# First loads in a fixed order, a mask on GpSimd, a gate factor in output rows, w_out in freed buffers, and the memory stage later

## Chip, cores and metric

One core of a Trainium2 chip runs the kernel. The metric is the device time of one execution in microseconds (us). TensorE is called PE here, VectorE DVE, ScalarE ACT, GpSimd POOL and SyncE SP; all DMAs of this kernel are issued by SP.

## What is computed

One layer of a decoder trunk for 2048 prompt tokens and 64 sample tokens of width 1024. In short:

```
z = rmsnorm(x) @ w_in          # columns: a_x | a_o | a_i, a_f | b_u | b_g
u = b_u * sigmoid(b_g)         # head group B: conv of width 31, layernorm, silu
ha = sigmoid(a_o) * headnorm(mlstm(conv4(a_x), a_i, a_f), a_hnorm)   # head group A
x = x + concat(ha, cb) @ w_out
mk, mv = rmsnorm(mem) @ x_wk, rmsnorm(mem) @ x_wv                    # 256 memory tokens
x = x + cross_attention(rmsnorm(x), mk, mv) @ x_wo
x = rmsnorm(x + convffn(rmsnorm(x)))
```

The mLSTM works in chunks of 128 tokens. Inside a chunk it needs, for each of 4 heads, a 128x128 matrix of decays: the exponential of a per-row term plus a per-column term, and zero above the diagonal. The output gate's sigmoid is computed as (tanh(x/2) + 1) / 2.

## The kernel before, in words

Every float32 product is three float32r matmuls (`mm3`, L153): each operand is split into a high part, an ACT cast or scaled copy, and a low part, a subtraction (`split`, L295). With a gain the low part is a scalar_tensor_tensor on DVE (L301); without one it is a subtraction on the engine that the caller names, DVE or POOL (L298).

**First pass** (loop at L588): 8 blocks of 256 tokens. `input_part` (L548) loads the rows, normalises and transposes them into the block's `h` (tiles `ha` and `hb` in turn) and stores `h` to DRAM. `gates_part` (L380) makes the gate columns, `gates_tm_part` (L393) turns them. `glu_part` (L406) makes b_u and b_g with the weights `wgt` and `wbv` (8 pieces of 256 KB each, `load_in` at L324, through 6 raw buffers) and stores `u`. In it ACT halves b_u into `hu` (L423), and DVE multiplies by tanh + 1 (L424). The tiles `tg`, `gT` and `ot` share one ring of two buffers, tag "tg" (L390, L418, L432); `ot` is stored to DRAM from its buffer (L435). `late_part` (L584, L366) loads and splits weights of the second pass in between. The tile `hb` lies where the raw buffers of the first loads lay (L578, L579). The first loads that the pass does not need at once are the small vectors (L563 to L570), the q, k, v maps (L453), and, in `first_loads` (L337), the gate columns and the conv states, which are transposed and stored again (`us`, L359).

**Second pass** (loop at L1273): `rest_part` (L1188) reads `h` back and makes a_x and the output gate (`wa`, `wo_` in pools wp2, wp2b); the gate tile `tg` gets (tanh + 1) times half the head-norm gain on DVE (L1222) and goes to DRAM; `head_out` (L728) multiplies it in. `pre_part` (L1246) calls `decay` (L761): 4 scalar_tensor_tensor on DVE per chunk add the per-row term and take the minimum with a mask tile `cap` (L764), then one ACT exponential of 128x512 (L768). `recur` (L781) is the chain from chunk to chunk. `conv_block` (L663) is the width-31 conv: ACT products, POOL additions (`cside`, L646), DVE scalar_tensor_tensor (`psG`, L648). `head_tail` uses DVE, ACT and POOL.

**The end of the second pass.** After the last `rest_part` (ch == 7, L1278) the pool wa2 closes. `memory_kv` (L984), the stage that makes mk and mv, then runs step by step inside the last chunks (`fold` in `steps`, L1265), and w_out is loaded in 16 pieces through 2 raw buffers into pools opened there (L1156 to L1161, L1282, L1302). `out_part` (L1173) is the product with w_out for 128 tokens, 17 in all: 14 in the loops at L1296 and L1308, then the sample tokens and two more (L1313, L1579, L1587) beside the **fold** of the attention weights (`fold_values` L1127, `fold_keys` L1073). Attention and the feed-forward follow.

The order on each engine and on the DMA queue is set at build time by the Tile framework, which takes instructions by program order and by a simulated timeline. `high_priority` (L560) puts a block first.

Of the kernel before, what the change touches and what calls it, by code (L numbers as in the profile page):

```python
# [33 lines left out]
FOLD_STEPS = 1, 1, 2  # L34
# [7 lines left out]
WO_FIRST = 4  # L42
# [54 lines left out]
def trunk_kernel(ctx: ExitStack, tc: tile.TileContext, i: dict, o: list):  # L97
# [231 lines left out]
    for j in range(2):  # L329
        SY.dma_start(b8[:, j, :4], i["a_bi"][0].partition_broadcast(P))  # L330
        SY.dma_start(b8[:, j, 4:], i["a_bf"][0].partition_broadcast(P))
# [74 lines left out]
    def glu_part(ch, xts, h, n):  # L406
        if ch == 0:
            pgs = [mmps() for _ in range(H)]
            for k in range(KT):
                for c in range(H):  # L410
                    gemm_k(pgs[c], wgt, c * P, h, n, k)
        for c in range(H):
            if ch == 0:
                pg = pgs[c]
            else:
                pg = mmps()
                gemm_fm(pg, wgt, c * P, h, n)
# [34 lines left out]
    for j, key in enumerate(("a_wq", "a_wk", "a_wv")):  # L452
        SY.dma_start(wqkv[:, j], i[key][0].rearrange("h d e -> d h e"))  # L453
# [94 lines left out]
    def input_part(ch):  # L548
        xts = xts0 if ch == 0 else load_x(lambda t: xp[t * P:(t + 1) * P, :], xs, ch)
# [5 lines left out]
        n = CH + (S if ch == 0 else 0)  # L555
        for z in range(2):
            SY.dma_start(h_d[ch][:, :, z], f(h[:, z, :, :n]))
        return ch, xts, h, n
# [3 lines left out]
    wgt = load_in(1032 + DA, W_FIRST)  # L562
# [25 lines left out]
    for ch in range(NCH):  # L588
        cur_ = cur
        gates_part(*cur)  # L590
        if ch:
            glu_part(*cur)
            gates_tm_part(*cur)
        if ch + 1 < NCH:
            cur = input_part(ch + 1)
        if ch == 0:
            glu_part(*cur_)
            gates_tm_part(*cur_)
# [92 lines left out]
    h2p = wa2.enter_context(tc.tile_pool(name="h2", bufs=H2_BUFS, side="right", reuse_waits="tile"))  # L691
    ut2 = wa2.enter_context(tc.tile_pool(name="ut2", bufs=2, side="right", reuse_waits="tile"))
# [9 lines left out]

    cap = const01(m1, [P, P], "cap", 0.0, [([[1, P]], -1, 0, GE, NEG)])
# [24 lines left out]
    def head_out(nd, nt, to_src, cat, pool):  # L728
# [5 lines left out]
        tt(to, to, pt[:, :H * nt].rearrange("p (h t) -> p h t", h=H), ALU.mult)  # L734
# [26 lines left out]
    def decay(dm, k, q, pm, a, nt, capt, qi=None):  # L761

        for hh in range(H):
            stt(dm[:nt, hh, :nt], pm[:nt, hh * nt:(hh + 1) * nt], a[:, hh:hh + 1], capt, ALU.add, ALU.min)  # L764
# [3 lines left out]
        act(dm[:nt, :, :nt], dm[:nt, :, :nt], AF.Exp)  # L768
# [26 lines left out]
    def sample_mlstm():  # L795
# [4 lines left out]
        with tc.tile_pool(name="smp", bufs=1, reuse_waits="tile") as smp:  # L800
# [3 lines left out]
            cap_s = const01(smp, [S, NB, NS], "cap_s", 0.0, [(*x, NEG) for x in samb])  # L804
# [351 lines left out]
    def out_pool(name, k0, k1):  # L1156
        return wos.enter_context(tc.tile_pool(name=name, bufs=2 * (k1 - k0), side="right", reuse_waits="tile"))

    def load_out(wpo, k0, k1):
        return [load_w(wpo, i["w_out"][0][k * P:(k + 1) * P, :], eng=G, raws=(wpo0, 2))  # L1160
                for k in range(k0, k1)]  # L1161
# [22 lines left out]
    fold = memory_kv()  # L1184
# [3 lines left out]
    def rest_part(ch):  # L1188
# [29 lines left out]
        for c in range(H):  # L1218
# [3 lines left out]
            ts(tg[:, :n], tg[:, :n], 1.0, ALU.add, hnh[:, c:c + 1], ALU.mult)  # L1222
# [23 lines left out]
    def pre_part(ch, j):  # L1246
# [7 lines left out]
        decay(dm, k[:, :, c], q[:, :, c], mrs[ch][:, j], av[:, t], P, cap, qi)  # L1254
# [17 lines left out]
    outs = list(range(NT - 2))  # L1272
    for ch in range(NCH + 2):  # L1273
# [4 lines left out]
        if ch == NCH - 1:  # L1278
            wa2.close()
            wpo0 = out_pool("wpo0", 0, WO_FIRST)  # L1280
            next(fold)
            wout = load_out(wpo0, 0, WO_FIRST)  # L1282
        for j in range(2):
# [12 lines left out]
            if ch == NCH + 1:  # L1296
                for _ in range(2):
                    out_part(outs.pop(0))
        if ch == NCH:
            for _ in fold:  # L1300
                pass
            wout += load_out(out_pool("wpo1", WO_FIRST, KT), WO_FIRST, KT)  # L1302
            ctp = wos.enter_context(tc.tile_pool(name="ctp", bufs=CT_BUFS, side="right", reuse_waits="tile"))
# [4 lines left out]
    while outs:  # L1308
        out_part(outs.pop(0))
        steps(0)  # L1310
    for _ in side:
        pass
    ahead = [out_load(t) for t in (NT, NT - 2)]  # L1313
    out_part(NT, ahead[0])
# [262 lines left out]
    pps = banks("A", "A", "G", "D", "E")  # L1577
    with tc.tile_pool(name="fv", bufs=1, reuse_waits="tile") as fv:
        out_part(NT - 2, ahead[1])  # L1579
# [7 lines left out]
        out_part(NT - 1)  # L1587
        for j, _ in enumerate(fold):
            if j == ROWS_AT:
                next(keys)  # L1590
    next(keys)
    wos.close()
    wfs = ExitStack()
# [326 lines left out]
```

## Time and profile before

| | |
|---|---|
| median of 3 runs | 3009.47 us (3009.05 to 3010.59) |
| profiled execution, its own time | 3008.2 us |
| its span, first to last instruction | 3006.2 us |
| mean granted TensorE clock | 0.968 |
| PE busy | 2815.6 us (94%) |
| DVE busy | 2179.5 us (72%) |
| ACT busy | 1536.3 us (51%) |
| POOL busy | 1115.3 us (37%) |

Times are counted from the span's start. A row of the windows view gives, for a stretch, the time each engine was busy in it (with the number of instructions), the TensorE clock granted (1.00 is full speed), the mean busy share of the 16 DMA engines and what they moved. "PE x <- ACT y" means that PE stood idle before an instruction that writes x until ACT had made y.

### The profile page before, as it was taken

Reading aid. Unit: us, or ns where it says so; the run is one execution under the profiler, and the core shown is the slowest. Engines: PE = TensorE matmul, PEld = TensorE weight load, DVE = VectorE, ACT = ScalarE, POOL = GpSimd, SP = SyncE. Lnnn points to the kernel's source line nnn. Section 1 sums busy time; section 2 is a strip of 40 time slices with the busy share of each in tenths; the row PEclk is TensorE's granted clock in tenths of the full one; section 3 lists DMA queues with packets and bytes.
Section 4 is the critical chain, followed back from the end, with each engine's and each line's share of the span. In section 5 each row is a group of like instructions: output and inputs, shape, how many; then the busy total and the mean of one; then the engine's idle time right before and its main releaser. Section 6 shows DMA issues by size and latency. Waiting matters only on the chain.

```text
span 3006.2 us, 49437 instructions
## 1 busy us (share of the span) xinstructions
PE 2815.6 (94%) x17924; PEld 2483.7 (83%) x17924; DVE 2179.5 (72%) x4022; ACT 1536.3 (51%) x3115; POOL 1115.3 (37%) x1299
## 2 busy tenths in 40 slices
PE   5798989989999889899989999999999999999998
PEld 4687889987787778766678898899989999899987
DVE  3478899986212688844498889877797777877776
ACT  3467657777201565522364445655466545544443
POOL 2338745444310352533352323433253322522222
PEclk8898999999899999999989999999999999999999
DMA  7343333345644622556864454655465544644442
GB/s 194 104 150 114 126 114 118 110 127 189 204 156 150 226 73 95 200 178 224 275 213 155 155 173 152 219 163 161 137 225 163 160 151 148 190 135 127 129 122 75
DMA packets 336940, 471.81 MB, mean 157 GB/s; under 512 B 33421, under 2 KB 238707, under 8 KB 336688
## 3 DMA queue, kind: packets, MB, share of 16 engines
q1 hardware_dynamic: 336696, 468.66, 48.8%
q8 instruction: 141, 2.31, 0.3%
q14 instruction: 103, 0.84, 0.1%
HBM read 361.68 MB, written 107.26 MB: 156 GB/s over the span
## 4 chain that ended last, share of the span: by engine, by line
PE 70%; DVE 14%; DMA 8%; issue 3%; ACT 2%; POOL 2%; SPq 1%; DVEq 0%; POOLq 0%; ACTq 0%
PE psA L151 20%; PE psD L151 15%; PE psF L151 14%; PE psE L151 9%; PE psG L151 9%; DVE psG L125 3%; DMA raw<-in_f_wup 2%; DVE wt L128 2%; DMA raw<-in_w_in 1%; PE psB L148 1%; PE psC L148 1%; DMA h<-h 1%; DVE acc L125 1%; DVE raw L128 1%; DVE dm L125 1%
## 5 line engine op out<-in xcount | busy, mean ns | idle before, releaser
L297 ACT CAST wt<-raw 128x512 fp32r<-128x512 f32 x888 | 539.1, 620 | 545.2 <-PE psA L151 149.7
L128 DVE TENSOR_TENSOR wt<-raw,wt 128x512 fp32r<-128x512 f32 x662 | 511.9, 790 | 107.8 <-ACT wt L297 103.4
L128 POOL TENSOR_TENSOR wt<-raw,wt 128x512 fp32r<-128x512 f32 x226 | 319.9, 1420 | 718.7 <-ACT wt L297 603.8
L151 PE MATMUL psA<-R,wt 128*128 128x256 f32 (+1 forms) x2448 | 335.1, 287 | 2.9 <-DVE R L125 1.6
L151 PEld LDWEIGHTS psA<-R,wt 128*128 128x128 f32 x2448 | 315.2, 191 | 6.1 <-DVE R L125 1.8
L128 POOL TENSOR_TENSOR cside<-cside,cprod 128x512 f32<-128x512 f32 (+2 forms) x248 | 251.5, 1015 | 137.5 <-ACT cprod L120 94.4
L125 DVE SCALAR_TENSOR_TENSOR psG<-ue,vc,psG 128x512 f32<-128x512 f32 (+2 forms) x448 | 256.9, 573 | 13.3 <-ACT psG L120 5.6
L151 PE MATMUL psA<-wt,ht 128*128 128x512 f32 (+1 forms) x768 | 192.1, 396 | 0.0
L151 PE MATMUL psD<-R,wt 128*128 128x256 f32 (+1 forms) x1248 | 178.3, 288 | 11.6 <-DVE R L128 4.2
L151 PE MATMUL psF<-R,wt 128*128 128x256 f32 (+1 forms) x1248 | 177.8, 287 | 2.5 <-DVE R L125 1.7
L151 PE MATMUL psE<-R,wt 128*128 128x256 f32 (+1 forms) x1224 | 173.8, 287 | 4.0 <-DVE u L128 2.5
L151 PEld LDWEIGHTS psD<-R,wt 128*128 128x128 f32 x1248 | 163.7, 191 | 15.5 <-DVE R L128 5.4
L151 PE MATMUL psG<-R,wt 128*128 128x256 f32 (+1 forms) x1224 | 174.9, 287 | 0.9 <-ACT R L120 0.5
L151 PEld LDWEIGHTS psA<-wt,ht 128*128 128x128 f32 (+1 forms) x768 | 141.5, 186 | 35.1 <-DVE u L128 0.2
L151 PEld LDWEIGHTS psF<-R,wt 128*128 128x128 f32 x1248 | 162.5, 189 | 4.3 <-DVE R L125 1.9
L151 PEld LDWEIGHTS psE<-R,wt 128*128 128x128 f32 x1224 | 159.0, 189 | 7.2 <-DVE u L128 3.3
L120 ACT ACTIVATE cprod<-ue,vc 128x512 f32<-128x512 f32 (+2 forms) x248 | 146.3, 603 | 32.0 <-POOL cside L128 30.9
L151 PEld LDWEIGHTS psG<-R,wt 128*128 128x128 f32 x1224 | 159.9, 190 | 2.0 <-ACT R L120 0.8
L125 DVE SCALAR_TENSOR_TENSOR y<-fe,vc,y 128x512 f32<-128x512 f32 x176 | 130.7, 779 | 14.2 <-ACT y L120 14.1
L151 PE MATMUL psA<-wf,l 128*128 128x512 f32 x516 | 129.8, 399 | 10.1 <-DVE u L128 5.9
L128 POOL TENSOR_TENSOR y<-y,u 128x256 f32<-128x256 f32 x110 | 98.6, 906 | 106.2 <-DVE u L128 89.5
L151 PEld LDWEIGHTS psA<-wf,l 128*128 128x128 f32 x516 | 95.9, 190 | 37.8 <-issue 13.2
(608 smaller groups left out, 6154.1 us busy)
## 6 DMA issues: line engine op xcount, KB each, us to landing
raw<-sum SPq DMA_DIRECT2D x132, 512.0 KB
raw<-in_f_wup SPq DMA_DIRECT2D x110, 512.0 KB
raw<-in_f_wdown SPq DMA_DIRECT2D x88, 512.0 KB
xt<-x SPq DMA_DIRECT2D x48, 512.0 KB
sum<-raw SPq DMA_DIRECT2D x44, 512.0 KB
raw<-in_f_wup SPq DMA_DIRECT2D x66, 256.0 KB
xt<-in_x_prompt SPq DMA_DIRECT2D x32, 512.0 KB
x<-xt SPq DMA_DIRECT2D x32, 512.0 KB
```

What stands on the lines that cost most here:

```text
L120: A.activation(out, in_, func, bias=bias, scale=scale)
L125: V.scalar_tensor_tensor(out=out, in0=in0, scalar=s, in1=in1, op0=op0, op1=op1)
L128: (eng or V).tensor_tensor(out=out, in0=a, in1=b, op=op)
L148: T.transpose(out, in_, ident[:n, :n])
L151: T.matmul(out, lhsT, rhs, start=start, stop=stop)
L297: A.copy(hi, src)
```

## The change

- **First loads.** After the first block's input, `wgt`, `wbv` and the rows of block 1 (`x_next`) are issued in program order on SP. Everything else of the first loads is tied behind the last of them: the store of the first `h`, the gate biases, the q, k, v maps, the small vectors, the gate columns, the conv states. Half of the low parts of `wgt` move from POOL to DVE. `wbv` carries the factor 0.5, so that the ACT copy into `hu` goes and DVE reads PSUM.
- **First pass.** `gT` and `ot` get rings of their own, and the next block's `input_part` stands ahead of this block's `glu_part`, which stands ahead of the gates.
- **Decay mask.** One affine select of 128x512 on POOL per chunk takes the place of the 4 DVE instructions; the per-row term becomes the bias of 4 ACT exponentials of 128x128.
- **Output gate.** The DVE instruction on the gate tile goes; `head_out` adds the 1 in its multiply; the head-norm gain goes into the first 4 of 8 row blocks of w_out, whose low parts are then made on DVE.
- **w_out** goes into the buffers of wp2 and wp2b as they come free; only its 2 raw buffers and `ct` need new room.
- **Memory stage.** `memory_kv` leaves the last chunks. One `out_part` per half chunk stands there instead, 8 remain, 4 of them between the steps of `memory_kv`, which runs before the fold, then the sample's and one, and 3 beside the fold.

```diff
-    def load_in(c0, n_pool=W_POOL):
-        return [load_w(wp1, w_in[k * P:(k + 1) * P, c0:c0 + DA], DA, raws=(rawp, N_RAW),
+    def load_in(c0, gain=None, n_pool=W_POOL):
+        return [load_w(wp1, w_in[k * P:(k + 1) * P, c0:c0 + DA], DA, gain=gain, raws=(rawp, N_RAW),
...
-        gTs[ch] = gT = ut.tile([P, CH + S], F32, name="gT", tag="tg")[:16]
+        gTs[ch] = gT = ut.tile([P, CH + S], F32, name="gT", tag="gT", bufs=1)[:16]
...
-            act(hu[:, :n], pu[:, :n], AF.Copy, scale=0.5)
-            stt(hu[:, :n], tg[:, :n], 1.0, hu[:, :n], ALU.add, ALU.mult)
+            stt(hu[:, :n], tg[:, :n], 1.0, pu[:, :n], ALU.add, ALU.mult)
...
-                ot = ut.tile([S, P], F32, name="ot", tag="tg")
+                ot = ut.tile([S, P], F32, name="ot", tag="ot")
...
+    def ordered(*args, **kw):
+        ins = plain_dma(*args, **kw)
+        tc.keep_in_program_order(ins)
+        in_order.append(ins)
+        return ins
...
-    wgt = load_in(1032 + DA, W_FIRST)
+    SY.dma_start = ordered
+    wgt = load_in(1032 + DA, n_pool=2)
+    wbv = load_in(1032, 0.5)
+    x_next = load_x(lambda t: xp[t * P:(t + 1) * P, :], xs, 1)
+    SY.dma_start = plain_dma
+    behind = tc.issue_after(in_order[-1].ins)
+    behind.__enter__()
+    keep_h(0, cur[2])
+    for j in range(2):
+        SY.dma_start(b8[:, j, :4], i["a_bi"][0].partition_broadcast(P))
+        SY.dma_start(b8[:, j, 4:], i["a_bf"][0].partition_broadcast(P))
+    for j, key in enumerate(("a_wq", "a_wk", "a_wv")):
+        SY.dma_start(wqkv[:, j], i[key][0].rearrange("h d e -> d h e"))
...
-    wbv = load_in(1032)
...
     first_loads()
+    behind.__exit__(None, None, None)
...
-        gates_part(*cur)
-        if ch:
-            glu_part(*cur)
-            gates_tm_part(*cur)
         if ch + 1 < NCH:
             cur = input_part(ch + 1)
+        glu_part(*cur_)
+        gates_part(*cur_)
+        gates_tm_part(*cur_)
...
-        tt(to, to, pt[:, :H * nt].rearrange("p (h t) -> p h t", h=H), ALU.mult)
+        stt(to, to, 1.0, pt[:, :H * nt].rearrange("p (h t) -> p h t", h=H), ALU.add, ALU.mult)
...
-        for hh in range(H):
-            stt(dm[:nt, hh, :nt], pm[:nt, hh * nt:(hh + 1) * nt], a[:, hh:hh + 1], capt, ALU.add, ALU.min)
+        dv = dm[:nt, :, :nt]
+        pmv = pm[:nt, :H * nt].rearrange("p (h t) -> p h t", h=H)
+        if capt is None:
+            G.affine_select(out=dv, in_=pmv, pattern=[[0, H], [1, nt]], compare_op=GE, fill=NEG, base=0, channel_multiplier=-1)
+        else:
+            tt(dv, pmv, capt[:, None, :].to_broadcast([nt, H, nt]), ALU.min)
...
-        act(dm[:nt, :, :nt], dm[:nt, :, :nt], AF.Exp)
+        for hh in range(H):
+            act(dv[:, hh], dv[:, hh], AF.Exp, bias=a[:, hh:hh + 1])
...
+    def load_out():
+
+        out = []
+        for k in range(KT):
+            pool = wp2 if k < (KT + W2_EARLY) // 2 else wp2b
+            out.append(load_w(pool, i["w_out"][0][k * P:(k + 1) * P, :], raws=(wor, 2),
+                              gain=hnh[:, k:k + 1] if k < H else None, eng=G))
+        return out
...
-            ts(tg[:, :n], tg[:, :n], 1.0, ALU.add, hnh[:, c:c + 1], ALU.mult)
...
-        for _ in range(FOLD_STEPS[at]):
-            next(fold, None)
...
-            wa2.close()
-            wpo0 = out_pool("wpo0", 0, WO_FIRST)
-            next(fold)
-            wout = load_out(wpo0, 0, WO_FIRST)
+            wa3.close()
+            wor = wos.enter_context(tc.tile_pool(name="wor", bufs=2, side="right", reuse_waits="tile"))
+            ctp = wos.enter_context(tc.tile_pool(name="ctp", bufs=CT_BUFS, side="right", reuse_waits="tile"))
+            wout = load_out()
...
+            if ch >= NCH - 1:
+                out_part(outs.pop(0))
...
-    while outs:
+    while len(outs) > NT - TAIL_OUT:
         out_part(outs.pop(0))
         steps(0)
...
+    for j, _ in enumerate(memory_kv()):
+        if j % 2:
+            out_part(outs.pop(0))
+    out_part(NT)
     with tc.tile_pool(name="fv", bufs=1, reuse_waits="tile") as fv:
-        out_part(NT - 2, ahead[1])
+        out_part(outs.pop(0))
...
         for j, _ in enumerate(fold):
+            if outs:
+                out_part(outs.pop(0))
             if j == ROWS_AT:
                 next(keys)
+        while outs:
+            out_part(outs.pop(0))
```

## Rows read from the trace of the kernel before

**Rows 1.** Windows: stretch, length, busy PE, PEld, DVE, ACT, POOL, clock, DMA share, GB/s.
```profile
0.00:20.00 20.00, 7.03 (x27) 5.14 (x27) 5.30 (x13) 10.40 (x22) 8.24 (x24) 1.00 0.85 229
...
40.00:100.00 60.00, 25.34 (x137) 20.29 (x136) 17.72 (x38) 15.47 (x29) 5.75 (x6) 0.72 0.70 161
100.00:350.00 250.00, 218.86 (x1663) 205.57 (x1662) 189.03 (x421) 173.85 (x367) 152.64 (x196) 0.93 0.40 129
350.00:650.00 300.00, 278.25 (x2203) 270.23 (x2203) 271.87 (x526) 208.70 (x536) 140.13 (x175) 0.99 0.35 106
650.00:690.00 40.00, 27.72 (x165) 23.48 (x164) 39.89 (x106) 33.15 (x95) 27.38 (x53) 0.79 0.48 150
690.00:950.00 260.00, 259.58 (x1213) 204.70 (x1212) 78.24 (x170) 72.55 (x160) 62.27 (x49) 0.97 0.50 167
950.00:1010.00 60.00, 56.00 (x278) 45.88 (x277) 31.06 (x51) 24.47 (x44) 0.00 (x0) 0.97 0.85 293
1010.00:1080.00 70.00, 49.19 (x298) 43.65 (x297) 57.72 (x68) 50.28 (x89) 50.91 (x48) 0.85 0.38 125
1080.00:3007.00 1927.00, 1873.64 (x11841) 1647.22 (x11839) 1480.16 (x2619) 941.13 (x1761) 662.41 (x746) 0.99 0.51 163
```

**Rows 2.** Waits of PE from 0 to 100 us: total, times, longest.
```profile
PE psD L151 <- ACT tg L120: 11.1, 1, 11.1
...
PE psC L148 <- DVE hb L125: 9.5, 4, 6.7
PE psC L148 <- ACT xt L120: 9.0, 2, 8.7
```

**Rows 3.** Timeline of SP: start, time, instruction, what it moves.
```profile
44.42 2.06 SPq L359 DMA_DIRECT2D us<-xt  x4
46.52 1.01 SPq L268 DMA_DIRECT2D xt<-in_x_prompt  x2
```

**Rows 4.** Timeline of ACT; in brackets its idle time and what ended it.
```profile
54.29 1.06 ACT L122 ACTIVATE hb<-xt 128x1024 fp32r<-128x1024 f32 x1 [7.22 <-DMA xt<-in_x_prompt]
...
68.26 0.62 ACT L297 CAST wt<-raw 128x512 fp32r<-128x512 f32 x1 [6.28 <-DMA raw<-in_w_in]
...
85.40 0.44 ACT L120 ACTIVATE tg<-psD 128x320 f32<-128x320 f32 x1 [5.52 <-DMA out<-ot]
```

**Rows 5.** Windows: the stretch of the low clock.
```profile
55.00:90.00 35.00, 9.48 (x35) 6.62 (x36) 13.28 (x29) 10.97 (x22) 3.44 (x4) 0.51 0.84 196
```

**Rows 6.** Waits of PE from 100 to 350 us.
```profile
PE psA L151 <- ACT gT L391: 3.5, 2, 2.0
PE psD L151 <- ACT gT L391: 2.8, 1, 2.8
```

**Rows 7.** Groups by form, DVE, 350 to 700 us: busy us, mean ns, idle.
```profile
L125 DVE SCALAR_TENSOR_TENSOR dm<-mr,av,cap 128x128 f32<-128x128 f32 x64 | 31.9, 553 | 0.1
...
L134 DVE TENSOR_SCALAR tg<-tg,lnh 128x256 f32<-128x256 f32 x28 | 14.2, 508 | 0.0
```

**Rows 8.** Groups by form, ACT, 350 to 700 us.
```profile
L120 ACT ACTIVATE nd<-nd,hw 128x128 f32<-128x128 f32 x48 | 14.9, 412 | 1.6 <-POOL hw L128 1.6
...
L120 ACT ACTIVATE dm<-dm 128x512 f32<-128x512 f32 x16 | 10.2, 636 | 12.4 <-DVE dm L125 12.3
```

**Rows 9.** One line's instructions, L441, the select that makes the mask.
```profile
L441 POOL TENSOR_SCALAR_AFFINE_SELECT cap<-cap x1: 294/294/294, 340.9 to 340.9; 128x128 f32<-128x128 f32 x1
```

**Rows 10.** Groups by form, POOL, the whole span.
```profile
L128 POOL TENSOR_TENSOR cside<-cside,cprod 128x512 f32<-128x512 f32 x132 | 175.2, 1328 | 82.5 <-ACT cprod L120 57.2 <-DVE dm L128 19.7
```

**Rows 11.** Timeline of DVE: four decays in a row.
```profile
655.63 6.82 DVE L125 SCALAR_TENSOR_TENSOR dm<-mr,av,cap 128x128 f32<-128x128 f32 x4
...
676.79 1.12 DVE L125 SCALAR_TENSOR_TENSOR dm<-mr,av,cap 128x128 f32<-128x128 f32 x4
```

**Rows 12.** Timeline of SP: pieces of w_out, two at a time.
```profile
780.80 1.55 SPq L220 DMA_DIRECT2D raw<-in_w_out  x2
...
785.86 1.92 SPq L220 DMA_DIRECT2D raw<-in_w_out  x2
```

More of the change, by code (lines that the diff above doesn't have):

```diff
@@ L33 @@
 CONV_BLOCKS = [(0, 1, 12), (1, 2, 12), (3, 2, 12), (5, 2, 12), (7, 1, 12)]
-FOLD_STEPS = 1, 1, 2
+TAIL_OUT = 8
 MLSTM_STEPS = 2, 1, 1
@@ L41 @@
 KV_POOL = 2
-WO_FIRST = 4
 OUT_POOL = 10
@@ L322, in trunk_kernel @@
     ut = wa1.enter_context(tc.tile_pool(name="ut", bufs=2, side="right", reuse_waits="tile"))
-    def load_in(c0, n_pool=W_POOL):
-        return [load_w(wp1, w_in[k * P:(k + 1) * P, c0:c0 + DA], DA, raws=(rawp, N_RAW),
+    def load_in(c0, gain=None, n_pool=W_POOL):
+        return [load_w(wp1, w_in[k * P:(k + 1) * P, c0:c0 + DA], DA, gain=gain, raws=(rawp, N_RAW),
                        eng=G if k % n_pool == n_pool - 1 else V) for k in range(KT)]
     b8 = keep.tile([P, 2, 8], F32, name="b8")
-    for j in range(2):
-        SY.dma_start(b8[:, j, :4], i["a_bi"][0].partition_broadcast(P))
-        SY.dma_start(b8[:, j, 4:], i["a_bf"][0].partition_broadcast(P))
     wg = keep.tile([P, KT, 16], F32R, name="wg")
@@ L451, in trunk_kernel @@
     wqkv = mc.tile([P, 3, H, P], F32, name="wqkv")
-    for j, key in enumerate(("a_wq", "a_wk", "a_wv")):
-        SY.dma_start(wqkv[:, j], i[key][0].rearrange("h d e -> d h e"))
     wqk = mc.tile([P, H, P], F32, name="wqk")
@@ L548, in input_part @@
     def input_part(ch):
-        xts = xts0 if ch == 0 else load_x(lambda t: xp[t * P:(t + 1) * P, :], xs, ch)
+        xts = xts0 if ch == 0 else x_next if ch == 1 else load_x(lambda t: xp[t * P:(t + 1) * P, :], xs, ch)
         h = htile(ch)
@@ L554, in input_part, with keep_h @@
         make_h(xts, "g_mix", h, tps0 if ch == 0 else tps, ch == 0)
-        n = CH + (S if ch == 0 else 0)
+        if ch:
+            keep_h(ch, h)
+        return ch, xts, h, CH + (S if ch == 0 else 0)
+    def keep_h(ch, h):
         for z in range(2):
-            SY.dma_start(h_d[ch][:, :, z], f(h[:, z, :, :n]))
-        return ch, xts, h, n
+            SY.dma_start(h_d[ch][:, :, z], f(h[:, z, :, :h_d[ch].shape[3]]))
+    in_order = []
+    plain_dma = SY.dma_start
+    def ordered(*args, **kw):
[3 more added lines that the diff above has]
+        return ins
     with tc.high_priority():
         cur = input_part(0)
-    wgt = load_in(1032 + DA, W_FIRST)
+    SY.dma_start = ordered
[11 more added lines that the diff above has]
+        SY.dma_start(wqkv[:, j], i[key][0].rearrange("h d e -> d h e"))
     vc1 = cols["vc1"] = vec_cols("vc1", [
@@ L589, in trunk_kernel @@
         cur_ = cur
-        gates_part(*cur)
-        if ch:
-            glu_part(*cur)
-            gates_tm_part(*cur)
         if ch + 1 < NCH:
             cur = input_part(ch + 1)
+        glu_part(*cur_)
+        gates_part(*cur_)
+        gates_tm_part(*cur_)
         if ch == 0:
-            glu_part(*cur_)
-            gates_tm_part(*cur_)
             fold_qk()
@@ L690, in trunk_kernel @@
     wp2b = wa2.enter_context(tc.tile_pool(name="wp2b", bufs=KT - W2_EARLY, side="right", reuse_waits="tile"))
-    h2p = wa2.enter_context(tc.tile_pool(name="h2", bufs=H2_BUFS, side="right", reuse_waits="tile"))
-    ut2 = wa2.enter_context(tc.tile_pool(name="ut2", bufs=2, side="right", reuse_waits="tile"))
+    wa3 = ExitStack()
+    h2p = wa3.enter_context(tc.tile_pool(name="h2", bufs=H2_BUFS, side="right", reuse_waits="tile"))
+    ut2 = wa3.enter_context(tc.tile_pool(name="ut2", bufs=2, side="right", reuse_waits="tile"))
     while late:
@@ L701, in trunk_kernel @@
     G.memset(stt_t, 0.0)
-    cap = const01(m1, [P, P], "cap", 0.0, [([[1, P]], -1, 0, GE, NEG)])
     negi = m1.tile([S, S], F32, name="negi", bufs=1)
@@ L803, in sample_mlstm @@
             tri_s = const01(smp, [S, NB, NS], "tri_s", 1.0, [(*x, 0.0) for x in samb])
-            cap_s = const01(smp, [S, NB, NS], "cap_s", 0.0, [(*x, NEG) for x in samb])
+            cap_s = const01(smp, [S, NB, NS], "cap_s", -LOW, [(*x, NEG) for x in samb])
             inb = const01(smp, [S, NB], "inb", 1.0, [([[-NS, NB]], 1, 0, GE, 0.0), ([[NS, NB]], -1, NS - 1, GE, 0.0)])
@@ L1154, in trunk_kernel @@
     wos = ExitStack()
[L1156 to L1161, printed above, removed]
+    def load_out():
[5 more added lines that the diff above has]
+        return out
     def out_load(t):
@@ L1183, in trunk_kernel @@
     side = sample_mlstm()
-    fold = memory_kv()
     axe = {}
@@ L1253, in pre_part @@
         kw = m2.tile([P, H, P], F32, name="kw", tag="kw")
-        decay(dm, k[:, :, c], q[:, :, c], mrs[ch][:, j], av[:, t], P, cap, qi)
+        decay(dm, k[:, :, c], q[:, :, c], mrs[ch][:, j], av[:, t], P, None, qi)
         weighted_k(kw, k[:, :, c], P, ex[:, 1, t])
@@ L1267, in steps @@
             next(side, None)
-        for _ in range(FOLD_STEPS[at]):
-            next(fold, None)
     rest_part(0)
-    outs = list(range(NT - 2))
+    outs = list(range(NT))
     for ch in range(NCH + 2):
@@ L1295, in trunk_kernel @@
                 steps(2)
[L1296 to L1303, printed above, removed]
+            if ch >= NCH - 1:
+                out_part(outs.pop(0))
         if 0 < ch <= NCH:
@@ L1307, in trunk_kernel @@
             conv_block(*CONV_BLOCKS[CONV_AT[ch]])
-    while outs:
+    while len(outs) > NT - TAIL_OUT:
         out_part(outs.pop(0))
         steps(0)
[L1311 to L1314, printed above, removed]
     for _ in side:
@@ L1586, in trunk_kernel @@
         keys = fold_keys(pairs, mT, pps, banks("E", "F"))
-        out_part(NT - 1)
         for j, _ in enumerate(fold):
+            if outs:
+                out_part(outs.pop(0))
             if j == ROWS_AT:
                 next(keys)
+        while outs:
+            out_part(outs.pop(0))
     next(keys)
     wos.close()
+    wa2.close()
     wfs = ExitStack()
```

## The prediction

> **What bounds the kernel now.** I read the table of busy times first: PE is busy 94% of the span, the next engine 72%. So time can come only from PE's idle 190.6 us (3006.2 less 2815.6) and from stretches at the lower clock. Then the windows by stage [rows 1], to see where the idle time lies: 34.7 us between 40 and 100 us, 31.1 in the first pass after it (100 to 350), 21.8 and 12.3 in the second pass (350 to 650, 650 to 690), almost none from 690 to 950, 4.0 and 20.8 around the fold (950 to 1010, 1010 to 1080), 53.4 in all the rest. The change reaches only the part up to 1080. Then PE's waits in the first 100 us [rows 2]: 11.1 us for a gate tile, 9.5 and 9.0 for block 1's rows. The timelines say why. The rows of block 1 are issued only at 46.52, behind small writes of the conv states [rows 3], and ACT begins to square them at 54.29 after 7.22 us of waiting for the load. At 68.26 ACT has stood 6.28 us before a weight of the second pass, and block 1's `hb` behind it in ACT's queue [rows 4]. The gate tile at 85.40 waited for a store of `ot` to land, since both lie in one ring [rows 4]. In the second pass I looked at DVE, which is busy 271.9 of 300 us and then 39.9 of 40 [rows 1].
>
> The sum is made against the profiled execution, 3008.2 us, which lies 1.3 us under the median of the runs (3009.47).
>
> **1. The start.** Between 40 and 100 us PE loses 34.7 us, and 29.6 of them are the three waits named [rows 1, 2]. The change takes the cause of two and may ease the third. `ot` and `gT` get rings of their own, so no gate tile waits for a store. The rows of block 1 are issued straight behind the weights: the first block's rows (1.25 MB), 16 pieces of 256 KB and 1 MB more, 6.25 MB together, or 6.55 million bytes. At the 229 GB/s of the first 20 us [rows 1] that takes 29 us, so they land at about 32 us, not at 54. PE has work until about 50 us then as now, which covers that load. What is late next: block 1's `hb` lies over the raw buffers, and the small vectors use these last. They are issued behind the 2.6 MB store of the first `h`, another 11 us at the same rate, so `hb` can be written from about 45 us. Its transposes may hold PE up for some us, and a weight of the second pass may again stand in ACT's way, though on an emptier queue. The moved DMAs (2 stores, 4 bias loads, 3 maps, 12 small vectors, the states' loads and writes) are also moved past SP's queue; nobody needs them before 45 us but the gates and the conv. POOL gives up half of the low parts of `wgt`, which DVE can take, with 17.7 of 60 us busy. I leave 5 us of the 34.7: a gain of 29.7. The bounds are 34.7 and 10 (the two waits for block 1 stay, at 18.5, and some 6 us come for the gates). From 55 to 90 us the clock was at its lower level, 1.2 GHz, nearly throughout (0.51), after PE had done almost nothing for some us, and PE was busy 9.5 us in it [rows 5]; at the upper level that is 4.8. That goes as well: 4.6, bounds 0 and 4.6. Together **-34** (-39 to -10).
>
> **2. The rest of the first pass.** 32 ACT copies into `hu` go, off the way from PE to the store of `u`. PE's waits for the copy into `gT`, 3.5 and 2.8 us [rows 6], go with the ring and with the new order of gates and products. **-6**; bounds 0 (the wait moves to the next copy) and -15, half of the idle 31.1.
>
> **3. The second pass.** DVE loses 64 decays, 31.9 us, and the 28 gate instructions of the common form, 14.2 us [rows 7]; `head_out` costs the same as before. It then has 266 us of work in the 340 us in which it had 312 [rows 1]. ACT gets 64 exponentials of 128x128 in place of 16 of 128x512. The nearest rows are 412 and 636 ns [rows 8]: 26.4 less 10.2 is 16 us more, hidden as ACT is idle 98 of the 340 us. The select is not in the trace at 128x512. At 128x128 it takes 294 ns [rows 9], so one select costs between 0.29 us and the 1.33 of a two-input addition of 128x512 [rows 10]. I take four times the small one, 1.18 us, as columns cost time in the additions: 18.8 us more on POOL, which is idle 172 of the 340 us; both ends (4.7 and 21.3) are hidden alike. The four exponentials wait for it, and behind them the chunk's other ACT work; with two `dm` buffers that is early enough. PE is idle 34.1 us in the 340. DVE at 92% causes a part of it, the loads of `h` and the chain from chunk to chunk the rest. I take a third: **-12**; bounds 0 and -24.
>
> Here a row speaks against the new engine as well as for it. Four decays took 6.82 us while POOL ran without a pause, and 1.12 us elsewhere [rows 11]: DVE and POOL hold each other up. The selects are new work of that kind, and if each held DVE for its whole length, 18.8 of the 46.1 us freed would be lost and the gain would be 7. The Trainium skill, SBUF — State Buffer, "Who interferes with whom", says so: a DVE instruction with two SBUF inputs and a GpSimd instruction that reads SBUF exclude each other for a whole instruction. By that rule the sum would be 5 us higher than by the freed time alone; the row agrees with it. I keep 12, as the removed decays were themselves among the instructions held up (553 ns on average).
>
> **4. The last chunks.** w_out comes in 16 pieces through 2 raw buffers; two pieces take 5.06 us [rows 12], so all take 40 us after the last `rest_part`. The low parts of 8 pieces move to DVE; even at the 1.33 us of POOL's addition of that size [rows 10] they are 10.6 us, beside DVE's idle 182 of 260 us after 690. Until now `memory_kv` filled PE from about 690, with 12.3 us idle before [rows 1]. Now only `out_part` can fill it, and it needs all 8 row blocks. So PE's poor stretch gets longer by some us: **+7**. Bounds: 0 (the first products run as pieces land) and +28 (the idle 12.3 doubles, and 27.7 us of work at 0.79 fall to 0.5, which is 16 more). After it PE is full as before: 8 `out_part` stand in the last chunks and the same work follows.
>
> **5. Memory stage and fold.** From 690 to 950 PE was busy 259.6 of 260 us [rows 1], so the stage was not free there; moved, it costs PE the same time, covered by 4 `out_part`. If that cover failed, each of its 4 halves would wait for its weights. Both banks that it fills are those of `out_part`, so at 8 changes PE may wait for an ACT copy, at 0.64 us [rows 8] 5 us. Three `out_part` beside the fold can fill the 4.0 us before 1010 and a little behind; `fold_keys` still cannot write its tiles before the last `out_part`. **-2**; bounds -8 and +5.
>
> Sum: -34 - 6 - 12 + 7 - 2 = -47, so 2961 us on the profiled execution's scale, 2962 as a median.
>
> **The rivals.** *All of it carries.* PE alone is the bound to 1080: the ends -39, -15, -24, 0 and -8 make -86, 2922; nearer to what a real schedule does, 2935. For: PE is the busiest engine everywhere. Against: idle time had several causes in each stage.
> *The start is given back.* DVE, POOL and ACT carry the convs and are busy 272, 140 and 209 of 300 us from 350 on; what PE gains early it then waits for them. If only 10 us of the start and nothing of part 2 last: -10 - 12 + 7 = -15, 2993. For: DVE at 91%. Against: DVE is idle 61 us from 100 to 350 and can begin earlier, since `u` comes earlier.
> *Slower: the selects come late.* POOL works in order, and a select can stand behind the conv's additions of 1.33 us each [rows 10]. Three of them make it 4 us late; where the chain from chunk to chunk waits for it, 16 chunks cost 64 us, and 2961 becomes 3025. It decides from 47 / 16 = 2.9 us per chunk. For: POOL's additions themselves once waited 19.7 us for a decay product on DVE [rows 10], so such queues do meet. Against: the select needs only rows loaded a block ahead.
> *The order does not hold.* The planner may place block 1's transposes or the weights otherwise than issued, so that part 1 brings nothing: -47 + 34 = -13, 2995.
>
> **How the numbers follow.** Forecast 0.60, all carries 0.15, given back 0.13, selects late 0.07, order fails 0.05. A measurement of this kernel tells about 0.2%, 6 us, from no change. The first three are faster, and half of the last; the other half of it is split between no change and slower. So faster 0.89, same 0.03, slower 0.08. The range 2925 to 2996 leaves out the late selects and the far end of "all carries".
>
> **What would show it.** Right: block 1's rows read before 40 us, PE idle under 10 us between 40 and 100, the clock at its upper level there; DVE's share from 350 on under 85% and PE's waits for `stt_t` shorter; some 15 us idle at the start of the last chunks; no gap where `memory_kv` runs. Wrong: PE waiting for `hb` or the gate columns at 45 to 70 us, PE waiting for `dm` behind POOL, a gap of 25 us or more before the first `out_part`, or a fold longer than 130 us.

## The result, and the profile after

The changed kernel takes 2965.93 us (median of 4 runs, 2963.25 to 2971.32), against 3009.57 for the kernel before: a ratio of 0.9857, 95% interval 0.984 to 0.9874. The profiled execution took 2968.27 us, its span is 2966.6, its mean granted clock 0.972 (before 0.968). The forecast was 2962. PE is busy 2807.9 us (95%), DVE 2142.2, ACT 1534.5, POOL 1109.8.

The windows of the changed kernel by the stages of [rows 1]; columns: stretch, length, busy PE, PEld, DVE, ACT, POOL, clock, DMA share, GB/s:

```profile
0.00:20.00 20.00, 9.75 (x39) 7.68 (x40) 11.20 (x19) 12.96 (x24) 9.47 (x24) 1.00 0.77 237
...
40.00:100.00 60.00, 48.31 (x327) 44.03 (x328) 23.45 (x64) 23.70 (x52) 9.34 (x13) 0.89 0.69 155
100.00:350.00 250.00, 233.95 (x1844) 225.61 (x1843) 206.44 (x475) 175.38 (x368) 159.57 (x211) 0.97 0.46 149
350.00:650.00 300.00, 276.54 (x2157) 261.71 (x2156) 259.32 (x513) 240.11 (x678) 174.07 (x229) 0.98 0.39 119
650.00:690.00 40.00, 39.09 (x178) 29.28 (x176) 15.13 (x36) 11.82 (x25) 7.42 (x8) 0.91 0.50 158
690.00:950.00 260.00, 238.24 (x1015) 184.79 (x1014) 75.52 (x125) 66.77 (x117) 37.91 (x24) 0.91 0.53 183
950.00:1010.00 60.00, 46.67 (x305) 41.66 (x303) 39.71 (x53) 32.79 (x63) 22.54 (x21) 0.97 0.53 176
```

Three things differ. From 40 to 100 us PE is idle 11.7 us where it was idle 34.7, and from 100 to 350 us 16.1 where it was 31.1 [rows 1]. From 650 to 690 us it is nearly full. But from 690 to 950 us, where it stood still for 0.4 us before, it is now idle 21.8 us at a mean clock of 0.91. A stretch holds other work in each kernel, since all comes earlier, so two points of the work are compared too: PE's last product of a first-pass `hb` with the weights of b_u or b_g, which marks the end of the first pass, and its first score product. They start at 278.9 and 1025.7 us after the change and at 339.9 and 1066.0 before it. The lead is 61 us at the end of the first pass and 40 at the first score product. Some 20 us are given back between them.

What PE waits for in the changed kernel from 40 to 100 us (total, times, longest), beside [rows 2]:

```profile
PE psA L150 <- ACT hb L119: 5.4, 3, 2.6
PE psC L147 <- DVE vc L197: 2.9, 1, 2.9
```

The gate tile's 11.1 us and the 8.7 us for block 1's rows are gone. Then the stretch around the memory stage: windows of the changed kernel (80 us at a low clock, and a gap), SP's timeline at the gap, and the first instruction of PE's timeline behind it (in brackets the idle time before it and what ended it):

```profile
670.00:750.00 80.00, 75.00 (x293) 53.96 (x292) 24.36 (x61) 14.39 (x33) 12.85 (x6) 0.81 0.45 148
770.00:790.00 20.00, 5.38 (x23) 2.85 (x23) 5.40 (x13) 10.54 (x18) 6.63 (x4) 0.57 0.87 313
```

```profile
746.56 22.51 SPq L1201 DMA_DIRECT2D x<-xt  x3
769.49 0.32 SPq L748 DMA_DIRECT2D cat<-to  x1
770.17 0.39 SPq L1330 DMA_DIRECT2D out<-ha  x1
...
771.85 0.36 SPq L1008 DMA_DIRECT2D xt<-in_mem_prompt  x1
```

```profile
781.88 0.48 PE L147 MATMUL psD<-ident,xt 128*128 128x128 f32 x1 [10.72 <-ACT xt L119]
```

PE finishes the sample tokens' last products at 771 us and then has nothing to do until the memory rows are there. SP asks for these only at 771.85, behind three stores of `x` that wait for products with w_out to be made and added, the sample tokens' rows and the state outputs. Load and normalising take until 781.88.

### The profile page after: what moved, and what is told of

It reads as the page before. It is cut to its first block, busy times and chain, and to the rows that moved or that the text cites. A ratio compares the mean times of both kernels' runs of the same rounds, so it can differ in the third digit from the quotient of the medians.

```text
span 2966.6 us, 49315 instructions
## 1 busy us (share of the span) xinstructions
PE 2807.9 (95%) x17924; PEld 2479.4 (84%) x17924; DVE 2142.2 (72%) x3937; ACT 1534.5 (52%) x3134; POOL 1109.8 (37%) x1299
## 4 chain that ended last, share of the span: by engine, by line
PE 72%; DVE 14%; DMA 6%; issue 4%; ACT 2%; POOL 1%; SPq 1%; DVEq 0%; POOLq 0%; ACTq 0%
PE psA L150 21%; PE psD L150 14%; PE psF L150 14%; PE psE L150 9%; PE psG L150 9%; DVE psG L124 2%; DMA raw<-in_f_wup 2%; DVE wt L127 2%; PE psC L147 1%; PE psB L147 1%; DVE raw L127 1%; DVE acc L124 1%; DVE u L127 1%; DVE wf L127 1%; DMA xt<-x 1%
## 5 line engine op out<-in xcount | busy, mean ns | idle before, releaser
L296 ACT CAST wt<-raw 128x512 fp32r<-128x512 f32 x872 | 528.8, 620 | 529.2 <-PE psA L150 150.6
L127 POOL TENSOR_TENSOR wt<-raw,wt 128x512 fp32r<-128x512 f32 x212 | 306.5, 1449 | 703.9 <-ACT wt L296 572.2
L150 PEld LDWEIGHTS psD<-R,wt 128*128 128x128 f32 x1248 | 163.7, 191 | 10.4 <-DVE R L127 3.8
L150 PE MATMUL psA<-wf,l 128*128 128x512 f32 x516 | 132.2, 404 | 10.8 <-DVE u L127 5.8
```

The source lines that it names most:

```text
L127: (eng or V).tensor_tensor(out=out, in0=a, in1=b, op=op)
L150: T.matmul(out, lhsT, rhs, start=start, stop=stop)
L296: A.copy(hi, src)
```

## Experiments

All runs were made beside the kernel before, whose medians lay between 3008.15 and 3011.32 us. The table has each kernel's median, its ratio to before with the 95% interval, and PE's idle time in four stretches of its profile (length less busy time). "Pass order" is the new order of the first pass's loop: the next block's input, then this block's products, then the gates.

| kernel | median us | ratio (interval) | 40–100 | 100–350 | 350–690 | 690–950 |
|---|---|---|---|---|---|---|
| before | 3009.57 | 1 | 34.7 | 31.1 | 34.0 | 0.4 |
| the change | 2965.93 | 0.9857 (0.984–0.9874) | 11.7 | 16.1 | 24.4 | 21.8 |
| b_load: loads in order | 3005.79 | 0.9986 (0.9977–0.9995) | 21.6 | 33.2 | 32.5 | 1.8 |
| b_rings: rings | 2984.80 | 0.9909 (0.989–0.9927) | 14.3 | 29.5 | 39.3 | 3.2 |
| b_pass: pass order | 2970.89 | 0.9872 (0.9856–0.9889) | 21.1 | 15.0 | 30.4 | 5.4 |
| b_order: rings, pass order | 2949.86 | 0.9799 (0.978–0.9819) | 8.8 | 16.4 | 28.7 | 2.7 |
| b_start: parts 1, 2 | 2946.09 | 0.9795 (0.978–0.9811) | 11.9 | 17.3 | 24.4 | 10.0 |
| b_second: part 3 | 2996.72 | 0.9961 (0.9947–0.9975) | 35.2 | 31.7 | 22.2 | 2.3 |
| s_both: parts 1, 2, 3 | 2946.56 | 0.9787 (0.9768–0.9807) | 10.4 | 16.5 | 21.0 | 8.7 |
| b_tail: parts 4, 5 | 3038.47 | 1.0101 (1.0086–1.0116) | 35.1 | 31.4 | 34.3 | 22.3 |
| a_nostart: parts 3, 4, 5 | 3018.61 | 1.0036 (1.0023–1.0049) | 35.0 | 32.3 | 19.4 | 22.4 |
| a_fill: change, one product in the gap | 2962.34 | 0.9839 (0.9816–0.9863) | 11.9 | 16.5 | 22.4 | 18.5 |
| a_rows: a_fill, rows earlier | 2959.54 | 0.9837 (0.9813–0.986) | 11.6 | 16.6 | 21.6 | 16.7 |
| a_again: the change | 2964.82 | 0.9849 (0.9825–0.9872) | 10.9 | 15.2 | 24.1 | 22.2 |

### Which part gains, which loses

Four kernels take the change apart. b_start is the kernel before with the hunks of the diff on `load_in`, `gT`, `hu`, `ot`, the ordered loads and the pass loop, and nothing else:

> The kernel before with the first loads in order, the rings of gT and ot and the order of the first pass (parts 1 and 2), nothing else. Theory A, read from the two traces (the first pass ends at 279 us after the change and at 345 before it; PE's idle time up to there falls from 79 to 31 us): the earlier end carries to the end of the kernel and only the moved memory stage gives time back. Then this kernel alone gains 45 to 60 us, 2950 to 2965, as much as the whole change or more. Rival B: the second pass cannot use the early start, DVE and the chain of chunks eat it up; then it gains 15 to 25 us, 2985 to 2995, with more waits of PE for DVE between 280 and 650 us.

It gained 62 us, a little over theory A's range. The first pass ends at 278.1 us instead of 339.9, the first score product comes at 1003.3 instead of 1066.0, so a lead of 62 us is still 63 us there. Nothing of it is lost in between.

b_second has the decay, the gate and the gain in w_out's rows:

```diff
-        return [load_w(wpo, i["w_out"][0][k * P:(k + 1) * P, :], eng=G, raws=(wpo0, 2))
+        return [load_w(wpo, i["w_out"][0][k * P:(k + 1) * P, :], eng=G, raws=(wpo0, 2),
+                       gain=hnh[:, k:k + 1] if k < H else None)
```

> The kernel before with the decay on GpSimd and the gate factor in the output rows (part 3, with the gain in w_out's row blocks), nothing else. Theory A: PE's idle time between the end of the first pass and the first product with w_out fell only from 34 to 30 us in the changed kernel, so this part is worth about 4 us, 3002 to 3009. Rival, the prediction's term: 12 us, 2994 to 3000. In this kernel DVE is freed from the old, late start, so it could also be worth more here than in the whole change.

It gained 11.4 us, the prediction's term and not theory A's 4.

b_tail has `wa3`, `load_out` without the gain, and the later memory stage:

> The kernel before with w_out in the buffers of the second pass and the memory stage later (parts 4 and 5), nothing else. Theory A: this part gives time back by itself. In the changed kernel PE is idle 14.6 of the 20 us from 770 to 790, behind the load of the memory rows, and runs at a granted clock of about 0.8 from 670 to 750; so this kernel is 15 to 30 us slower than before, 3025 to 3040. Rival: the stretch is poor only because the first pass came earlier (the stores and the sample steps then crowd it); then it is within 8 us of before, 3002 to 3017. The prediction's terms for the two parts make +5, 3014.

It lost 30.3 us by itself, at the upper end of theory A. Its profile has the gap of the changed kernel, later, as all is later (PE waits 10.7 us for the memory rows there too); the windows of b_tail there:

```profile
740.00:800.00 60.00, 59.08 (x245) 42.30 (x245) 19.85 (x53) 9.77 (x23) 7.14 (x7) 0.80 0.46 136
840.00:870.00 30.00, 14.77 (x62) 10.20 (x61) 7.95 (x17) 12.02 (x21) 6.72 (x5) 0.66 0.74 267
```

So the gap and the low clock do not come from the earlier start.

a_nostart is the changed kernel with the hunks of b_start taken back:

> The changed kernel without parts 1 and 2 (first loads, rings and first pass as before). Theory A: it loses what the start alone brings, 45 to 60 us, 3011 to 3026, slower than the kernel before. Rival B: it loses 15 to 25, 2981 to 2991. Prediction's terms: 40 us, 3006.

At 3018.61 us it is slower than the kernel before, by 0.36% (0.23% to 0.49%), inside theory A's range. Without the start the change is a loss. Beside parts 4 and 5, part 3 is worth 19.9 us (3038.47 less 3018.61).

s_both puts the two gaining parts together (the hunks of b_start and b_second):

> Parts 1, 2 and 3 together (start, first pass, decay and gate factor), with w_out and the memory stage as before. If the parts add, as the runs so far suggest (62 us for the start, 11 for the second pass, 30 given back by the tail), it gains 73 us: 2935, the fastest of all. Rival: with the start put right, PE's idle time in the second pass hangs on the chain from chunk to chunk and on the loads of h, not on DVE; then the second part adds under 5 us and the kernel stays at 2942 to 2947.

The rival held: 2946.56 us, no better than b_start by anything these runs can tell, as the intervals lie over each other. PE's waits for `stt_t` are shorter (6.6 us against 11.5), and it is idle less from 350 to 690 us (21.0 against 24.4), but its clock from 690 to 950 us is 0.95 where b_start has 0.98, and from 950 to 1010 us 0.83 where it has 0.89. What part 3 frees is lost again by then: the first score product starts at 1004.6 us, against 1003.3 in b_start. Why the clock is lower there stays open. The separate gains do not add where part 3 is concerned: 62 and 11 alone, 64.8 together. What it is worth within the whole change no run shows.

### What in the start brings it

b_load orders the first loads alone:

```diff
-    wgt = load_in(1032 + DA, W_FIRST)
+    wgt = load_in(1032 + DA, n_pool=2)
+    wbv = load_in(1032)
+    x_next = load_x(lambda t: xp[t * P:(t + 1) * P, :], xs, 1)
```

> The kernel before with the first loads in order alone (and half of the first low parts on DVE); rings, halving copy and order of the first pass as before. Theory: the late rows of block 1 and the transfers in front of them are most of the start's loss; 35 to 45 us, 2963 to 2973. Rival: hb lies over the raw buffers and the ring shared with ot still stops the gate tile, so the early rows bring little without the rings and the new order; 10 to 18 us, 2990 to 2998.

It gained 4 to 6 us (ratio 0.9986), less than even the rival said. One reason is a new hole: in b_load's timeline PE stands still before the small vectors, whose loads now stand behind the weights, block 1's rows, the biases and the maps,

```profile
39.21 0.33 PE L148 MATMUL psC<-ident,raw 60*128 60x60 f32 x1 [10.36 <-DMA raw<-in_f_conv_b]
```

and behind them in PE's queue stand the gate columns and then the products of `glu_part`, whose weights had long been there. In the old pass order the gates come first. So PE is idle 10.8 us from 20 to 40 us, where it was never idle before the change, and 13.1 us less than there from 40 to 100. There it still waits 9.9 us for `hu`, whose copy stands in ACT's queue behind a weight of the second pass, and 8.7 us for gate tiles:

```profile
67.29 1.14 ACT L297 CAST wt<-raw 128x512 fp32r<-128x512 f32 x2 [11.57 <-DMA raw<-in_w_in]
68.33 0.43 ACT L120 ACTIVATE hu<-psA 128x320 f32<-128x320 f32 x1
```

b_rings gives `gT` and `ot` rings of their own:

```diff
-        gTs[ch] = gT = ut.tile([P, CH + S], F32, name="gT", tag="tg")[:16]
+        gTs[ch] = gT = ut.tile([P, CH + S], F32, name="gT", tag="gT", bufs=1)[:16]
...
-                ot = ut.tile([S, P], F32, name="ot", tag="tg")
+                ot = ut.tile([S, P], F32, name="ot", tag="ot")
```

> The kernel before with rings of their own for gT and ot alone. Theory: the wait of 11.1 us for a gate tile and the 6.3 us for the copy into gT go, and a part of them is found again behind the late rows; 5 to 12 us, 2996 to 3003. Rival: the 11.1 us were only the last of several waits at the same place, the late load of block 1 stays the bound; under 4 us, 3004 or more.

26.5 us, three times the middle of the theory's range. Not only the 11.1 us for the gate tile went: the wait for block 1's `xt` fell from 9.0 to 4.4 us and the clock from 40 to 100 us rose from 0.72 to 0.89, though SP asks for these rows at 45.28 us, hardly before the 46.52 of the kernel before [rows 3].

```profile
40.00:100.00 60.00, 45.73 (x332) 42.32 (x331) 22.23 (x50) 23.14 (x45) 5.68 (x7) 0.89 0.75 172
100.00:350.00 250.00, 220.55 (x1660) 207.97 (x1658) 198.71 (x454) 173.22 (x374) 152.30 (x197) 0.96 0.41 133
```

The profiled execution took 2992.05 us, the other three 2978.95 to 2985.41. In it the first pass ends at 303.7 us, 36 us earlier than in the kernel before, and the first score product starts at 1049.1, only 17 us earlier: with the rings alone, a good half of the lead was given back in between. PE is idle 39.3 us from 350 to 690 us there, the most of all these kernels.

b_pass changes the loop alone:

```diff
-        gates_part(*cur)
-        if ch:
-            glu_part(*cur)
-            gates_tm_part(*cur)
         if ch + 1 < NCH:
             cur = input_part(ch + 1)
+        glu_part(*cur_)
+        gates_part(*cur_)
+        gates_tm_part(*cur_)
```

> The kernel before with the new order of the first pass alone: the next block's input ahead of this block's products, these ahead of the gates; rings and loads as before. Rings and this order together gained 60.8 us, the rings alone 26.5. If the two add, the order alone brings 30 to 38 us, 2973 to 2981. Rival: with gT, tg and ot in one ring of two buffers the new order still stops at the stores of ot, so that it brings under 20 us, 2991 or more, and needs the rings to pay.

39.1 us, a little over the range of the first case (the two add): the largest single piece. It works in both stretches; the windows of b_pass:

```profile
40.00:100.00 60.00, 38.94 (x214) 33.34 (x212) 17.93 (x40) 19.63 (x38) 5.59 (x7) 0.77 0.73 157
100.00:350.00 250.00, 234.97 (x1848) 226.13 (x1847) 201.86 (x461) 172.53 (x372) 151.44 (x195) 0.97 0.43 141
```

From 100 to 350 us PE's waits for the copy into `gT` (3.5 and 2.8 us [rows 6]) are not there any more, and those for `hb`, 7.2 us in the kernel before, are 2.7: the next block's transposes are issued ahead of this block's products, and ACT and DVE make its `h` beside these.

b_order has b_rings' and b_pass's edits together, and no ordered loads:

> The kernel before with the rings of gT and ot and the new order of the first pass, but with the first loads issued as before and the halving copy kept. Alone, the ordered loads gained 5.5 us and the rings 26.5; all of the start gained 62. Theory: ordered loads pay only where the products of b_u and b_g stand ahead of the gates, since the gate columns come last in that order; then this kernel lacks 15 to 30 us of the 62 and stands at 2962 to 2978. Rival: the ordered loads bring nothing anywhere, rings and pass order are the whole start; then 2947 to 2955.

The rival held: 60.8 us, against 62.1 for the whole start. With these two the ordered loads, the DVE share of the low parts and the dropped copies into `hu` add nothing that can be measured. The timelines show why. In the changed kernel SP asks for block 1's rows at 20.00 us and ACT begins to square them into `hb` at 50.51 (b_start has 20.16 and 50.32):

```profile
20.00 0.90 SPq L560 DMA_DIRECT2D xt<-in_x_prompt  x2
```

```profile
49.20 0.57 ACT L119 ACTIVATE psG<-ue,vc,vc 128x256 f32<-128x256 f32 x1 [4.79 <-DMA ue<-u]
...
50.51 1.04 ACT L121 ACTIVATE hb<-xt 128x1024 fp32r<-128x1024 f32 x1
```

```profile
44.26 0.24 PE L147 MATMUL psC<-ident,raw 88*128 88x88 f32 x1
```

In b_order SP asks at 41.06, and ACT begins at 50.34:

```profile
41.06 2.33 SPq L268 DMA_DIRECT2D xt<-in_x_prompt  x2
```

```profile
50.34 1.06 ACT L122 ACTIVATE hb<-xt 128x1024 fp32r<-128x1024 f32 x1 [2.21 <-DMA xt<-in_x_prompt]
```

The rows are asked for 21 us earlier and wait: `hb` lies over the raw buffers, PE reads the last of the small vectors from these at 44.26 us, and then ACT has stood 4.79 us before a conv product in front of `hb` in its queue, which waits for its load of `u`. Whether early rows would pay with another order on ACT was not tried.

### Can the tail be mended

a_fill puts a product with w_out, loaded ahead, between the load of the memory rows and their transposes:

```diff
+    ahead = out_load(outs[0])
     for _ in side:
         pass
...
+    kv = memory_kv()
+    next(kv)
+    out_part(outs.pop(0), ahead)
```

> The changed kernel with one of its products with w_out, its operand loaded beforehand, between the load of the memory rows and their transposes. Theory: PE's idle 14.6 us from 770 to 790 is the load and the normalising of the memory rows, which SP issues behind the sample tokens' last stores; a product of 11 us in it gives 8 to 12 us, 2954 to 2958. Rival: the gap only moves, to the weights of the memory stage or to the fold, which has one product less beside it; then within 4 us of the changed kernel, 2962 to 2970.

The product ran ahead of the transposes, but the rows came no earlier, and PE still waited 7.5 us for them. The median of 2962.34 lies at the edge of the rival's range, with runs from 2953.87 to 2969.42: no gain that can be told from the change.

a_rows also asks for the rows ahead of the sample tokens' last steps:

```diff
+    ahead = out_load(outs[0])
+    load_rows()
     for _ in side:
         pass
```

> The changed kernel with the memory rows loaded ahead of the sample tokens' last steps, and one product with w_out ahead of their transposes. With the product alone the gap of 10.7 us before the transposes became 7.5, as the rows came no earlier. Theory: the rows' place in SP's queue is the cause; with both, PE waits under 3 us for the rows, and the kernel gains 8 to 14 us on the changed kernel beside it, 2952 to 2958. Rival: the weights of the memory stage, issued behind the same stores, are late next; the gap stays at 6 us or more and the gain is under 5 us.

The wait for the rows fell to 2.4 us, as the theory said; from the timeline of a_rows (SP's line is the second of the two loads):

```profile
753.86 0.33 SPq L1007 DMA_DIRECT2D xt<-in_mem_prompt  x1
```

```profile
777.59 0.33 PE L147 MATMUL psD<-ident,xt 128*128 128x128 f32 x1 [2.39 <-ACT xt L119]
...
783.58 0.69 PE L147 MATMUL psD<-ident,xt 128*128 128x128 f32 x2 [4.51 <-DVE hm L124]
```

But the next step, the low part of `hm`, is late in its place (4.51 us), and from 690 to 950 us PE is idle 16.7 us instead of 22.2 beside it. The kernel gained 5 us on a_again, under the theory's 8 to 14, and the intervals overlap. So the rows' place in SP's queue causes the long wait that PE shows, but ending it returned some 5 us of the 30, not clear of the spread of the runs. Most of the loss seems to lie elsewhere.

> The changed kernel itself, beside the others on the same chip: 2963 to 2971, as in its first runs.

a_again came out at 2964.82 (2959.49 to 2973.09), as before, and shows how far single runs spread.

Part 4 without part 5 was not tried, so how the 30 us divide between the two parts stays open. The fastest kernels are not versions of the whole change: b_start and b_order, which leave parts 3 to 5 alone, are faster than both kernels, with intervals (0.978 to 0.9811, and 0.978 to 0.9819) clear of the change's.

## Why the prediction was right, and where not

The time was right, and so was its sign, but by luck. The sum of -47 was met at -43.6 because two errors of over 20 us each cancelled: measured alone, parts 1 and 2 brought 22 us more than their terms, and parts 4 and 5 cost 25 more.

**Parts 1 and 2 (-34 and -6; measured together 62).** The step that failed is "The rows of block 1 are issued straight behind the weights": I took their late issue [rows 3] for the cause of two of the three waits. The 62 us lie beyond even the far ends of both terms, 39 and 15. Issuing them early brings 4 to 6 us alone and, with the rest of the ordered loads, nothing measurable on top of rings and pass order. I had written myself that `hb` lies over the raw buffers and can be written only from about 45 us. The raw buffers were read until 44.5, and ACT came to `hb` at 50.5, behind a conv product. Neither hangs on the rows. What carried was priced at almost nothing: the pass order, as part of the 6 us of part 2, alone brought 39; the rings, as the 11.1 us of one wait, brought 26.5. The row that should have said so is the idle 31.1 us from 100 to 350 [rows 1], of which I let half be the bound: half is what went, but with it the clock there rose from 0.93 to 0.97. "nobody needs them before 45 us but the gates and the conv" named the right danger and did not follow it: in the old order the gates stand ahead of everything (b_load's 10.36 us).

**Part 3 (-12; measured -11.4 alone).** The sum was right for the kernel before and did not carry onto the earlier start (s_both), where nothing measurable was left. Its pieces: the select, whose price was unknown, and the four exponentials, from groups of the changed kernel (min, median, max in ns, and mean):

```profile
L779 POOL TENSOR_SCALAR_AFFINE_SELECT dm<-mr x16: 625/638/1149, 288.0 to 616.3; 128x512 f32<-128x512 f32 x16
```

```profile
L119 ACT ACTIVATE dm<-dm,av 128x128 f32<-128x128 f32 x62 | 19.8, 403 | 0.1
```

The select took 0.638 us at the median where I took 1.18, the exponential 403 ns on average against 412. DVE is busy 259.3 of 300 us from 350 on, 86% (I had said under 85). PE's waits for `stt_t`, 11.8 us before, are 8.2 in the changed kernel and 4.7 in b_second. The conv's instruction on DVE, which reads SBUF once and `psG` in PSUM, takes 749 ns on average in the kernel before and 749 in b_second, beside the selects. The Trainium skill, SBUF — State Buffer, "Who interferes with whom", says that a DVE instruction with at most one SBUF input, outside the modes that use both ports, does not contend with GpSimd; the trace agrees, as far as this mean can show it. The removed decays, which read two tiles in SBUF, took 553 ns on average [rows 7] but 344 at the median, and up to 2712, so the freed time was partly time held up, as the prediction argued; that POOL held them up rests on [rows 11] alone. The rule's other sum, a gain of 7, is below the interval of b_second (7.5 to 15.9 us) by little.

**Parts 4 and 5 (+7 and -2; measured +30 alone, and some 20 on top of the other parts, as the whole change gains 43.6 and s_both 64.8).** The idle time at the start of the last chunks did not come: the first product with w_out starts at 613.9 us and PE is idle 0.9 us from 650 to 690. The step that failed is "moved, it costs PE the same time, covered by 4 `out_part`". Before the change the memory stage's products were what PE did between the small steps of the sample tokens; these then ran at full clock for the most part. Two lines of PE and two windows of the kernel before show it: with products of the memory stage (`hm`) between the 8-column products of the sample tokens (`c0T`) the clock is 1.00, and it falls once these are used up, behind 765 us:

```profile
752.22 1.40 PE L151 MATMUL psA<-q_s,c0T 128*128 128x8 f32 x12
753.47 0.72 PE L151 MATMUL psD<-wt,hm 128*128 128x512 f32 x2
```

```profile
750.00:760.00 10.00, 10.00 (x49) 7.44 (x47) 3.21 (x8) 3.10 (x5) 2.81 (x3) 1.00 0.75 230
...
770.00:780.00 10.00, 9.73 (x33) 6.86 (x31) 3.82 (x10) 3.90 (x6) 5.01 (x3) 0.50 0.84 269
```

In the changed kernel the sample steps have only products with w_out beside them, in long runs, and the clock is 0.81 for 80 us. That the products between the steps kept it up is argued from these lines; no run tests it. And the stage itself starts with a chain of load, norm and transposes that nothing covered, because SP's queue held its first load back. I had listed the queues that a moved DMA passes for part 1 and not for the memory rows.

**The rivals.** "The order does not hold" comes nearest in part 1: not that the planner changed it, but that it brought nothing. "The start is given back" fell: b_start keeps all of it, though b_rings alone does not. "All of it carries" fell with parts 4 and 5. The late selects did not come: PE's waits for `dm` are 3.1 us in the whole second pass, and those are for DVE's product. It is POOL that waited, 29.2 us before eight selects, until PE had read the `dm` buffer. The chances of "faster" add up to 0.905 by the rule given, not 0.89.

**What was to be seen.** Block 1's rows read before 40 us: no, 50.5. PE idle under 10 us from 40 to 100: nearly, 11.7. The clock at its upper level there: no, 0.89. A sign of being wrong came in a small size: PE waited 5.4 us for `hb`. No gap where `memory_kv` runs: wrong, 14.6 us from 770 to 790.

## What to carry to other kernels

Before a load is moved forward, find what its consumer writes into and what stands before that consumer in its engine's queue: where the tile lies over buffers that are still being read, an early load only waits. Where an engine's order is set at build time, what stands in front of ready work can be worth more than how early the data come: moving one block's input and products ahead of the gates was the largest single gain here, 39 us, against 4 to 6 for the early loads. Work that fills the idle time between small dependent steps is not free to move, even where its own price stays the same; when it goes, look for what fills those holes next, and for the stores in front of its first load.

## What the runs showed of the hardware

PE's clock fell while PE was busy. Windows of the changed kernel at one of the sample steps:

```profile
690.00:695.00 5.00, 5.00 (x24) 4.14 (x23) 0.69 (x1) 0.00 (x0) 0.00 (x0) 1.00 0.01 1
695.00:700.00 5.00, 4.76 (x31) 3.64 (x29) 2.28 (x4) 1.07 (x2) 0.00 (x0) 1.00 0.27 106
700.00:705.00 5.00, 4.36 (x20) 3.21 (x18) 3.73 (x10) 2.12 (x3) 0.21 (x1) 0.63 0.75 216
705.00:710.00 5.00, 5.00 (x16) 3.38 (x16) 0.78 (x4) 0.00 (x0) 2.14 (x1) 0.50 0.38 150
710.00:715.00 5.00, 5.00 (x10) 2.46 (x9) 1.69 (x7) 0.00 (x0) 0.00 (x0) 0.50 0.00 0
715.00:720.00 5.00, 5.00 (x16) 3.93 (x16) 0.00 (x0) 0.00 (x0) 0.00 (x0) 0.67 0.70 210
720.00:725.00 5.00, 5.00 (x24) 4.14 (x23) 0.69 (x1) 0.00 (x0) 0.00 (x0) 1.00 0.02 3
```

Before the fall PE ran the sample tokens' products, which are 8 columns wide, with pauses of 0.24 to 0.40 us:

```profile
696.71 1.95 PE L150 MATMUL psA<-q_s,c0T 128*128 128x8 f32 x16 [0.24 <-ACT c0T L967]
```

From 700 to 720 us it was idle 0.6 us by the profile, but the granted clock was 0.575 on average, at or near its lower level of 1.2 GHz: by estimate 8.5 us of full-speed work lost (20 times 0.425) that no idle time shows. The kernel before has the same fall where its last sample steps run with no other products between them (0.50 from 770 to 780 us).

One queue entry can hide a long stop: the three stores of `x` from 746.56 take 22.51 us together in SP's timeline, because each waits until DVE has added products that PE is still making, and the memory rows stand behind them.
